# RMS factors of a four-layer transformer: the broadcast copy left out, the squares summed later, and the reciprocal root on GpSimd

## The chip, the core and the metric

The kernel runs on one core of a Trainium2 chip. The core has five engines that work side by side from instruction queues of their own: TensorE (PE) for matmuls, VectorE (DVE), ScalarE (ACT), GpSimd (POOL) and SyncE (SP), which here only starts DMA transfers. The metric is the device time of one execution in microseconds (us); several executions are made, and their median counts.

## What is computed

Four transformer layers run over 512 tokens of width 1024, in float32. Two are hybrid layers, whose mixer joins chunked attention, a convolution module and a retention branch; two are layers with latent attention, whose two low-rank projections (ckv and cq) have RMS norms of their own. Every layer has an FFN of squared ReLU. What matters here is that each layer is framed by norms:

```python
def rms_norm(x, g):
    y = xf * lax.rsqrt(jnp.mean(xf * xf, axis=-1, keepdims=True) + EPS)
    return (y * g.astype(jnp.float32)).astype(x.dtype)

def hybrid_layer(x, ...):
    h = rms_norm(x, g_mix_pre)
    ...
    mix = jnp.concatenate([y_att, y_conv, y_ret], axis=-1) @ w_out
    x = x + rms_norm(mix, g_mix_post)
    h = rms_norm(x, g_mlp_pre)
    f = jnp.square(jax.nn.relu(h @ w_up)) @ w_down
    return x + rms_norm(f, g_mlp_post)
```

The convolution's and the retention's layer norms need a reciprocal root as well.

## The kernel before

**Layout.** The activations stand transposed: x is 8 tiles of 128 features x 512 tokens, so a norm is a sum over partitions and over 8 tiles. The weights come as chunks of 128x1024 by DMA from SP into `raw` (three buffers). ACT rounds each chunk to `wh` (L510) and DVE subtracts to get the rest, `wl` (L512). Every product is three matmuls: wh with the activation's high part hh, wh with its low part hl, wl with hh (L528 to L530 in `dense`, L545 to L547 in `lin_tok`).

**A norm.** ACT squares each tile and DVE adds the squares into one accumulator (`add_sq`, L676, L677). PE multiplies the accumulator by a column of 1/d, one matmul with one output column for 128 tokens, into a bank pc (L662, "the column sums" here). `rstd` (L629 to L643) makes the reciprocal root y of pc + EPS on DVE: v, a seed by an integer shift (L635, L636), and three Newton steps of three instructions each (L638 to L640): twelve instructions on 128 x 2, 4 or 8 elements. `bcast_rows` copies y, each token's value repeated 128 times, into a tile bt (DVE, L647), and PE transposes bt 128 columns at a time (L653): now the value of each token stands on every partition in a bank rb.

There are 32 such norms in the program. Ten are *factors* (`factor_parts`): the norm ahead of a projection is applied behind it, so the projection runs on x times gain meanwhile, and y is also copied to `rt` (L689) and rb to SBUF by ACT (L692). Ten are *halves*: the mixer's and, in the hybrid layers, the FFN's output is normed in two halves of 256 tokens (eight in `post_norm1`, and two for the program's output). Six are of the retention, two of the convolution, four of the latents ckv and cq.

**post_norm1.** Its `sink` takes each output tile into f (L991) and sums squares into acc. Its `done`, a generator, waits for the norm of a half, and then for each of the 8 tiles: f = f * gain * rb (DVE, L1005), x = x + f (DVE, L1007), the parts hh (ACT, L681) and hl (DVE, L682) of the next projection's input, and the squares of the new x into acc2 (ACT L676, DVE L677) for the factor that comes next. The consumer of hh and hl is the next projection's first half, on PE.

**Order.** The program is written as a stream of Python generators; a scheduler then sets the order of each engine's instructions by its own costs and due times. Each engine runs its own row in order and waits at semaphores. So an instruction that waits holds up what stands behind it on its engine.

Of the kernel before, what the change touches and what calls it, by code (L numbers as in the profile page):

```python
# [13 lines left out]
I32 = mybir.dt.int32  # L14
AF = mybir.ActivationFunctionType
ALU = mybir.AluOpType
# [46 lines left out]
CHAIN = 2  # L63
# [285 lines left out]

CONSTS = ("ident", "one1", "m256", "m64", "tri", "neg1", "identr", "smask", "vec", "cmpv")


class Normed:
# [8 lines left out]
class Prog:  # L364
    def __init__(self, nc, tc, es, A, out, plan):
# [18 lines left out]
        else:  # L384
            self.__dict__.update(dict.fromkeys(CONSTS, nc))
            self.ones = dict.fromkeys((1024, 256, 128), nc)
# [54 lines left out]
    def consts(self):  # L441
        nc, A = self.nc, self.A

        def c(nm, shape, dt=F32):
            return self.cst.tile(shape, dt, tag=nm, name=nm)

        self.ident = c("ident", [128, 128])
        make_identity(nc, self.ident)
        self.ones = {}
        for d in (1024, 256, 128):  # L450
            self.ones[d] = c(f"ones{d}", [128, 1])
            nc.vector.memset(self.ones[d], 1.0 / d)
        self.one1 = c("one1", [128, 1])
        nc.vector.memset(self.one1, 1.0)
        self.m256 = c("m256", [128, 128])
        nc.vector.memset(self.m256, 1.0 / 256)
        self.m64 = c("m64", [128, 128])
        nc.vector.memset(self.m64, 0.0)
        nc.vector.memset(self.m64[0:64, 0:64], 1.0 / 64)
        nc.vector.memset(self.m64[64:128, 64:128], 1.0 / 64)  # L460
        self.tri = c("tri", [128, 128], F32R)
        nc.gpsimd.memset(self.tri.bitcast(F32), -1.0)
        nc.gpsimd.affine_select(self.tri, self.tri, pattern=[[-1, 128]], compare_op=ALU.is_ge,
                                fill=0.0, base=0, channel_multiplier=1)
        self.neg1 = c("neg1", [128, 128], F32R)
        nc.gpsimd.memset(self.neg1.bitcast(F32), -1.0)
        self.identr = c("identr", [128, 128], F32R)
        nc.vector.tensor_copy(self.identr, self.ident)
        self.smask = c("smask", [128, 128], F32R)
        nc.gpsimd.memset(self.smask.bitcast(F32), NEG)  # L470
        nc.gpsimd.affine_select(self.smask, self.smask, pattern=[[-1, 128]], compare_op=ALU.is_ge,
                                fill=0.0, base=0, channel_multiplier=1)

        nc.scalar.activation(c("warm", [128, 1]), self.one1, AF.Copy)
        self.vec = c("vec", [128, NVEC])
        nc.sync.dma_start(self.vec, A["vec"])
        self.cmpv = c("cmpv", [128, 4])
# [151 lines left out]
    def rstd(self, pc, n):  # L629

        nc = self.nc
        v, y, a = (self.SM(x)[:, :n] for x in "vya")
        yi = y.bitcast(I32)
        nc.vector.tensor_scalar(v, pc, EPS, None, op0=ALU.add)
        nc.vector.tensor_scalar(yi, v.bitcast(I32), 1, None, op0=ALU.logical_shift_right)  # L635
        nc.vector.tensor_scalar(yi, yi, -1, 0x5F3759DF, op0=ALU.mult, op1=ALU.add)  # L636
        for _ in range(3):
            nc.vector.tensor_tensor(a, y, y, op=ALU.mult)  # L638
            nc.vector.scalar_tensor_tensor(a, a, -0.5, v, op0=ALU.mult, op1=ALU.mult)
            nc.vector.scalar_tensor_tensor(y, a, 1.5, y, op0=ALU.add, op1=ALU.mult)  # L640
        return y

    def bcast_rows(self, y, nt, g, bank=None):  # L643

        nc = self.nc
        bt = self.S(s="bt")
        nc.vector.tensor_copy(  # L647
            bt[:, :nt * 128].rearrange("p (n r) -> p n r", n=nt * g),
            y.rearrange("p (n o) -> p n o", o=1).to_broadcast([128, nt * g, 128 // g]))
        rb = (bank or self.ptr)(nt * 128)  # L650
        for t in range(nt):
            s = slice(128 * t, 128 * t + 128)
            nc.tensor.transpose(rb[:, s], bt[:, s], self.ident)  # L653
        return rb

    def mean_rstd(self, accs, d, t0=0, t1=512, bank=None):
# [327 lines left out]
    def post_norm1(self, xs, f, g_post, g_next):  # L984

        nc = self.nc
        acc, last, acc2, hd = self.S(s="acc"), self.S(s="last"), self.S(s="acc2"), Normed(self)

        def sink(i, o, ps, t0, t1):
            s = slice(t0, t1)  # L990
            nc.vector.tensor_tensor(f[o][:, s], ps, f[o][:, s], op=ALU.add)  # L991
            if i < 7:
                self.add_sq(acc[:, s], f[o][:, s], i == 0)
            else:
                nc.scalar.activation(last[:, s], f[o][:, s], AF.Square)

        def done(t0, t1):
            s = slice(t0, t1)
            y = self.mean_rstd([acc, last], 1024, t0, t1)
            yield  # L1000
            yield
            rb = self.bcast_rows(y, (t1 - t0) // 128, 1)
            yield
            for o in range(8):
                nc.vector.scalar_tensor_tensor(f[o][:, s], f[o][:, s], g_post[:, o:o + 1], rb,  # L1005
                                               op0=ALU.mult, op1=ALU.mult)
                nc.vector.tensor_tensor(xs[o][:, s], xs[o][:, s], f[o][:, s], op=ALU.add)  # L1007
                self.gained(xs[o], g_next, hd, o, t0, t1)
                self.add_sq(acc2[:, s], xs[o][:, s], o == 0)
                if o % CHAIN == CHAIN - 1:  # L1010
                    yield
            if t1 == 512:
                self.after = self.factor_parts(hd, [acc2], FACTOR_LAG)

        return sink, done, hd

    def residual2(self, xs, scale, g_next, final=False):
# [594 lines left out]
```

## Time and profile before

| | |
|---|---|
| median of 3 runs | 3307.41 us (3305.97 to 3307.50) |
| the profiled execution's own time | 3305.43 us |
| its span on the core | 3303.7 us |
| TensorE's granted clock, mean | 0.994 of full speed |
| PE busy | 3251.5 us, 98% of the span |
| DVE busy | 1964.7 us, 59% |
| ACT busy | 1345.8 us, 41% |
| GpSimd busy | 70.0 us, 2% |

The span is the time from the first to the last instruction of the profiled execution; 1.7 us of that execution lie around it. The page lists busy time of each engine, the chain of work that ended last, and groups of instructions. A timeline row gives the start, the length, the engine, the line of the code, the operation with its output and inputs, and in brackets how long the engine stood idle before it and what released it. Matmuls overlap in PE, so their lengths are longer than the distance of their starts, and the distance is the pace.

### The profile page before, as it was taken

How to read it: one execution, taken by the hardware profiler on the slowest of the kernel's cores; microseconds unless marked ns; L12 is line 12 of the kernel's file. 1: busy time of each engine (PE TensorE's matmuls, PEld its weight loads, DVE VectorE, ACT ScalarE, POOL GpSimd, SP SyncE). 2: the span in 40 equal slices, each digit the busy share in tenths (PEclk: the TensorE clock that was granted, in tenths of full speed). 3: DMA queues.
4: the chain of work that ended last, by engine and by line, in shares of the span. 5: the costliest groups of instructions: out<-in, count | busy, mean ns of one | idle time of the engine just before them, and what ended most of it. 6: DMA issues, size and time to landing. Idle time of an engine off the chain costs nothing.

```text
span 3303.7 us, 40955 instructions
## 1 busy us (share of the span) xinstructions
PE 3251.5 (98%) x15956; PEld 2673.1 (81%) x15956; DVE 1964.7 (59%) x3571; ACT 1345.8 (41%) x2254; POOL 70.0 (2%) x151
## 2 busy tenths in 40 slices
PE   8999999999999999999999999999999999999998
PEld 7888888887888888888877688888888877778887
DVE  6977334788734456454678664546445468664454
ACT  4454323546533333232566732323222357742222
POOL 0100000010000000000000000000000000000000
PEclk9999999999999999999999999999999999999999
DMA  5222222342122222222323032222222323222222
GB/s 176 95 71 89 97 101 96 119 137 83 65 102 96 96 96 101 98 96 96 117 85 120 20 106 99 96 96 96 96 96 97 121 79 106 68 77 96 96 96 70
DMA packets 100866, 317.27 MB, mean 96 GB/s; under 512 B 12608, under 2 KB 18112, under 8 KB 100672
## 3 DMA queue, kind: packets, MB, share of 16 engines
q1 hardware_dynamic: 100672, 314.66, 28.3%
q8 instruction: 125, 2.05, 0.2%
q14 instruction: 69, 0.57, 0.1%
HBM read 298.75 MB, written 6.29 MB: 92 GB/s over the span
## 4 chain that ended last, share of the span: by engine, by line
PE 90%; DVE 5%; ACT 2%; DMA 1%; issue 1%; SPq 0%; DVEq 0%; ACTq 0%
PE pd L528 12%; PE pd L529 12%; PE pd L530 12%; PE ps L530 6%; PE ps L528 6%; PE ps L529 6%; PE pt L528 6%; PE pt L529 6%; PE pt L530 6%; PE po L528 3%; PE po L530 3%; PE po L529 3%; PE po L777 3%; PE pt L745 2%; DVE wl L512 1%; PE ps L617 1%
## 5 line engine op out<-in xcount | busy, mean ns | idle before, releaser
L510 ACT ACTIVATE wh<-raw 128x1024 fp32r<-128x1024 f32 (+2 forms) x546 | 567.5, 1041 | 1356.9 <-PE pd L529 561.2
L512 DVE TENSOR_TENSOR wl<-raw,wh 128x1024 fp32r<-128x1024 f32 (+2 forms) x546 | 654.4, 1200 | 420.0 <-ACT wh L510 418.8
L528 PE MATMUL pd<-hh,wh 128*128 128x512 f32 (+1 forms) x1328 | 506.7, 385 | 7.4 <-ACT wh L510 3.7
L530 PE MATMUL pd<-hh,wl 128*128 128x512 f32 (+1 forms) x1328 | 505.3, 381 | 3.1 <-DVE wl L512 3.1
L529 PE MATMUL pd<-hl,wh 128*128 128x512 f32 (+1 forms) x1328 | 506.2, 382 | 0.4 <-DVE hl L682 0.2
L528 PEld LDWEIGHTS pd<-hh,wh 128*128 128x128 f32 x1328 | 249.0, 189 | 58.9 <-ACT hh L681 5.9
L530 PEld LDWEIGHTS pd<-hh,wl 128*128 128x128 f32 x1328 | 250.8, 189 | 49.1 <-DVE wl L512 3.3
L529 PEld LDWEIGHTS pd<-hl,wh 128*128 128x128 f32 x1328 | 250.9, 189 | 46.7 <-DVE hl L682 2.0
L530 PE MATMUL ps<-hh,wl 128*128 128x512 f32 (+1 forms) x528 | 196.7, 374 | 0.0
L529 PE MATMUL ps<-hl,wh 128*128 128x512 f32 (+1 forms) x528 | 196.3, 372 | 0.0
L528 PE MATMUL ps<-hh,wh 128*128 128x512 f32 (+1 forms) x528 | 196.1, 373 | 0.2 <-ACT wh L510 0.2
L528 PE MATMUL pt<-hh,wh 128*128 128x512 f32 x480 | 187.1, 391 | 0.6 <-ACT wh L510 0.6
L529 PE MATMUL pt<-hl,wh 128*128 128x512 f32 x480 | 187.3, 390 | 0.0
L530 PE MATMUL pt<-hh,wl 128*128 128x512 f32 x480 | 186.3, 389 | 0.0
L528 PE MATMUL pd<-ah,wh 128*128 128x512 f32 (+1 forms) x498 | 185.0, 372 | 0.0
L529 PE MATMUL pd<-al,wh 128*128 128x512 f32 (+1 forms) x498 | 184.8, 371 | 0.0
L530 PE MATMUL pd<-ah,wl 128*128 128x512 f32 (+1 forms) x498 | 184.8, 371 | 0.0
L586 ACT ACTIVATE ah<-sc 128x512 fp32r<-128x512 f32 x88 | 55.6, 632 | 180.9 <-DVE sc L1130 180.9
L529 PE MATMUL ps<-al,wh 128*128 128x512 f32 (+1 forms) x332 | 123.4, 372 | 0.0
L528 PE MATMUL pt<-ah,wh 128*128 128x512 f32 (+1 forms) x332 | 123.3, 371 | 0.0
L530 PE MATMUL ps<-ah,wl 128*128 128x512 f32 (+1 forms) x332 | 123.3, 371 | 0.0
L530 PE MATMUL pt<-ah,wl 128*128 128x512 f32 (+1 forms) x332 | 123.2, 371 | 0.0
(475 smaller groups left out, 6354.5 us busy)
## 6 DMA issues: line engine op xcount, KB each, us to landing
raw<-in_w SPq DMA_DIRECT2D x514, 512.0 KB
raw<-in_w SPq DMA_DIRECT2D x20, 384.0 KB
xd<-x SPq DMA_DIRECT2D x16, 256.0 KB
x<-xd SPq DMA_DIRECT2D x16, 256.0 KB
sw<-sc SPq DMA_DIRECT2D x48, 64.0 KB
ct<-in_ret SPq DMA_DIRECT2D x12, 256.0 KB
sn<-in_ret SPq DMA_DIRECT2D x12, 256.0 KB
mst<-in_bias SPq DMA_DIRECT2D x12, 256.0 KB
```

The lines of the kernel that those rows point to most:

```text
L510: nc.scalar.activation(h[:, :n], raw[:, :n], AF.Copy)
L512: eng.tensor_tensor(lo[:, :n], raw[:, :n], h[:, :n].bitcast(F32), op=ALU.subtract)
L528: mm(ps, h, rh[j][:, t0:t1], start=first and j == 0, stop=False)
L529: mm(ps, h, rl[j][:, t0:t1], start=False, stop=False)
L530: mm(ps, lo, rh[j][:, t0:t1], start=False, stop=last and j == n - 1)
L586: self.nc.scalar.activation(dst, src, AF.Copy, scale=scale)
L617: self.nc.tensor.matmul(ps, st, m[:, c], start=True, stop=False)
L745: nc.tensor.transpose(pt[:, o:o + 128], P[qt][:, 128 * kt:128 * kt + 128], self.ident)
L777: self.nc.tensor.matmul(po[a:a + 64, 128 * kt:512], v[kt][:, o + a:o + a + 64], pt[kt], start=start and kt == 0, stop=stop and kt == 3, sk ...
```

## The change

The functions `rstd`, `bcast_rows` and `post_norm1.done` change, and a constant tile of -0.5 (128x8) is added.

- `rstd`: v = pc + EPS stays on DVE. The root is then one GpSimd instruction, v to the power -0.5, and one Newton step follows on GpSimd in four instructions. Eleven DVE instructions go, five GpSimd instructions come, in all 32 norms.
- `bcast_rows`: for a norm with one group per token (26 of 32; the six retention norms have two groups) the copy bt goes. PE's transpose reads y itself, one column repeated 128 times.
- `post_norm1.done`: the squares of the new x are summed in a loop of their own behind the eight tiles, not tile by tile.

```diff
-CONSTS = ("ident", ...
+CONSTS = ("mhalf", "ident", ...
...
+        self.mhalf = c("mhalf", [128, 8])
+        nc.vector.memset(self.mhalf, -0.5)
...
         v, y, a = (self.SM(x)[:, :n] for x in "vya")
-        yi = y.bitcast(I32)
         nc.vector.tensor_scalar(v, pc, EPS, None, op0=ALU.add)
-        nc.vector.tensor_scalar(yi, v.bitcast(I32), 1, None, op0=ALU.logical_shift_right)
-        nc.vector.tensor_scalar(yi, yi, -1, 0x5F3759DF, op0=ALU.mult, op1=ALU.add)
-        for _ in range(3):
-            nc.vector.tensor_tensor(a, y, y, op=ALU.mult)
-            nc.vector.scalar_tensor_tensor(a, a, -0.5, v, op0=ALU.mult, op1=ALU.mult)
-            nc.vector.scalar_tensor_tensor(y, a, 1.5, y, op0=ALU.add, op1=ALU.mult)
+        nc.gpsimd.tensor_tensor(y, v, self.mhalf[:, :n], op=ALU.pow)
+        nc.gpsimd.tensor_tensor(a, y, y, op=ALU.mult)
+        nc.gpsimd.tensor_tensor(a, a, v, op=ALU.mult)
+        nc.gpsimd.tensor_scalar(a, a, -0.5, 1.5, op0=ALU.mult, op1=ALU.add)
+        nc.gpsimd.tensor_tensor(y, y, a, op=ALU.mult)
         return y
...
-        bt = self.S(s="bt")
-        nc.vector.tensor_copy(
-            ...
         rb = (bank or self.ptr)(nt * 128)
+        if g > 1:
+            bt = self.S(s="bt")
+            nc.vector.tensor_copy(
+                ...
         for t in range(nt):
             s = slice(128 * t, 128 * t + 128)
-            nc.tensor.transpose(rb[:, s], bt[:, s], self.ident)
+            nc.tensor.transpose(rb[:, s], bt[:, s] if g > 1 else y[:, t:t + 1].to_broadcast([128, 128]), self.ident)
...
                 self.gained(xs[o], g_next, hd, o, t0, t1)
+                if o % CHAIN == CHAIN - 1:
+                    yield
+            for o in range(8):
                 self.add_sq(acc2[:, s], xs[o][:, s], o == 0)
-                if o % CHAIN == CHAIN - 1:
+                if o % 4 == 3:
                     yield
```

The scheduler gives the new code a new order. The FFN bodies keep theirs; around the norms it changes. DVE's row goes from 3555 to 3178 instructions, GpSimd's from 123 to 287. This table, counted from the two orders, says how many matmuls stand on PE between a norm's last column sum and its first transpose (norms numbered in the order of the program):

| norms | before | after |
|---|---|---|
| factors 1; 8, 18, 21; 11 | 27; 30; 39 | 5; 8; 12 |
| factors 22, 27; 25, 30; 26 | 23; 25; 17 | 8; 8; 4 |
| first halves of a mixer 6, 16; of an FFN 9, 19 | 47; 43 | 24; 30 |
| second halves 7, 17; 10; 20 | 33; 49; 38 | 9; 6; 14 |
| halves of the output 31; 32 | 26; 0 | 11; 0 |
| ckv 23, 28; cq 24, 29 | 10; 20 | 4; 7 |
| conv 5; 15 | 19; 16 | 8; 8 |
| retention 2, 12; 3, 13; 4; 14 | 47; 47; 58; 48 | 26; 8; 31; 23 |

On PE at the ckv norm of the first latent layer (norm 23), before. `pd` is the bank of the norm, L617 and L618 transpose a state, L1249 applies attention weights:

```order
L662 MATMUL pd_13902<-ones_91,acc_13820 128x1 x4
L617 MATMUL ps_13943<-mh_13481,st_13730 128x128
L618 MATMUL ps_13943<-ml_13482,st_13730 128x128
L617 MATMUL pt_13954<-mh_13487,st_13733 128x128
L618 MATMUL pt_13954<-ml_13488,st_13733 128x128
L1249 MATMUL po_13641<-a_13889,v_13440 64x512
L1249 MATMUL po_13641<-a_13900,v_13440 64x512
L617 MATMUL ps_13971<-mh_13481,st_13730 128x256
L618 MATMUL ps_13971<-ml_13482,st_13730 128x256
L617 MATMUL pt_13982<-mh_13487,st_13733 128x256
L618 MATMUL pt_13982<-ml_13488,st_13733 128x256
L653 MATMUL pd_13924<-ident,bt_13922 128x128 x4
```

and after (lines of the changed kernel, one to four lines higher):

```order
L663 MATMUL pd_13740<-ones_91,acc_13658 128x1 x4
L619 MATMUL ps_13773<-mh_13319,st_13568 128x128
L620 MATMUL ps_13773<-ml_13320,st_13568 128x128
L619 MATMUL pt_13784<-mh_13325,st_13571 128x128
L620 MATMUL pt_13784<-ml_13326,st_13571 128x128
L654 MATMUL pd_13754<-ident,y_13746 128x128 x4
L1253 MATMUL po_13479<-a_13727,v_13278 64x512
L1253 MATMUL po_13479<-a_13738,v_13278 64x512
```

The transposes, which read y in place of bt, stand behind 4 matmuls in place of 10.

On DVE at the factor behind the mixer of layer 0 (norm 8), before. v to y are `rstd`, wl the rests of weight chunks:

```order
L634 TENSOR_SCALAR v_2850<-po_2845 128x4
L635 TENSOR_SCALAR y_2851<-v_2850 128x4
L636 TENSOR_SCALAR y_2851<-y_2851 128x4
L638 TENSOR_TENSOR a_2852<-y_2851 128x4
L639 SCALAR_TENSOR_TENSOR a_2852<-a_2852,v_2850 128x4
L640 SCALAR_TENSOR_TENSOR y_2851<-a_2852,y_2851 128x4
L638 TENSOR_TENSOR a_2852<-y_2851 128x4
L639 SCALAR_TENSOR_TENSOR a_2852<-a_2852,v_2850 128x4
L512 TENSOR_TENSOR wl_2686<-raw_2683,wh_2685 128x1024
L512 TENSOR_TENSOR wl_2744<-raw_2741,wh_2743 128x1024
L640 SCALAR_TENSOR_TENSOR y_2851<-a_2852,y_2851 128x4
L512 TENSOR_TENSOR wl_2942<-raw_2939,wh_2941 128x1024
```

(the last Newton step, rt and bt follow) and after:

```order
L635 TENSOR_SCALAR v_2802<-po_2797 128x4
L690 COPY rt_2176<-y_2803 128x4
L514 TENSOR_TENSOR wl_2634<-raw_2631,wh_2633 128x1024
L514 TENSOR_TENSOR wl_2680<-raw_2677,wh_2679 128x1024
L1106 SCALAR_TENSOR_TENSOR relu_2854<-pd_2542,rb_2175 128x512
L1106 SCALAR_TENSOR_TENSOR relu_2861<-pd_2543,rb_2175 128x512
L1106 SCALAR_TENSOR_TENSOR relu_2868<-ps_2544,rb_2175 128x512
```

Behind v stands at once `rt`, which reads the y of GpSimd; two wl that stood inside the norm's instructions stand behind it, and then the FFN's squared ReLU (L1106), which reads rb.

On DVE behind the mixer's first half in layer 0, before. acc_421 is acc2, the squares of the new x; acc_2188 is acc, those of f in the second half:

```order
L682 SCALAR_TENSOR_TENSOR hl_2201<-x_120,vec,hh_2193 128x256
L1005 SCALAR_TENSOR_TENSOR f_2100<-f_2100,vec,pt_2436 128x256
L677 TENSOR_TENSOR acc_421_2190<-acc_421_2190,sq_2489 128x256
L682 SCALAR_TENSOR_TENSOR hl_2202<-x_121,vec,hh_2194 128x256
L1007 TENSOR_TENSOR x_122<-x_122,f_2100 128x256
L677 TENSOR_TENSOR acc_421_2190<-acc_421_2190,sq_2496 128x256
L677 TENSOR_TENSOR acc_2188<-acc_2188,sq_2513 128x256
L682 SCALAR_TENSOR_TENSOR hl_2203<-x_122,vec,hh_2195 128x256
L1005 SCALAR_TENSOR_TENSOR f_2137<-f_2137,vec,pt_2436 128x256
L677 TENSOR_TENSOR acc_421_2190<-acc_421_2190,sq_2520 128x256
L1007 TENSOR_TENSOR x_123<-x_123,f_2137 128x256
L991 TENSOR_TENSOR f_1846<-po_2530,f_1846 128x256
```

and after:

```order
L1006 SCALAR_TENSOR_TENSOR f_2068<-f_2068,vec,pt_2396 128x256
L678 TENSOR_TENSOR acc_2156<-acc_2156,sq_2438 128x256
L683 SCALAR_TENSOR_TENSOR hl_2169<-x_122,vec,hh_2161 128x256
L1008 TENSOR_TENSOR x_124<-x_124,f_2068 128x256
L683 SCALAR_TENSOR_TENSOR hl_2170<-x_123,vec,hh_2162 128x256
L1006 SCALAR_TENSOR_TENSOR f_2105<-f_2105,vec,pt_2396 128x256
L678 TENSOR_TENSOR acc_2156<-acc_2156,sq_2463 128x256
L683 SCALAR_TENSOR_TENSOR hl_2171<-x_124,vec,hh_2163 128x256
L1008 TENSOR_TENSOR x_125<-x_125,f_2105 128x256
L992 TENSOR_TENSOR f_1822<-po_2474,f_1822 128x256
L1006 SCALAR_TENSOR_TENSOR f_2126<-f_2126,vec,pt_2396 128x256
L683 SCALAR_TENSOR_TENSOR hl_2172<-x_125,vec,hh_2164 128x256
```

The sums into acc2 have gone from between f, x and hl; in the changed program they stand behind the last hl of the half.

## Rows read from the trace of the kernel before

**Rows 1.** The page, section 1 (busy us, share of the span, instructions) and 4 (chain).
```profile
PE 3251.5 (98%) x15956; PEld 2673.1 (81%) x15956; DVE 1964.7 (59%) x3571; ACT 1345.8 (41%) x2254; POOL 70.0 (2%) x151
...
PE 90%; DVE 5%; ACT 2%; DMA 1%; issue 1%; SPq 0%; DVEq 0%; ACTq 0%
```

**Rows 2.** Timeline of PE; start us, us, engine line op out<-in [idle before <-releaser].
```profile
611.77 0.28 PE L530 MATMUL pd<-ah,wl 128*128 128x256 f32 x1
611.89 0.28 PE L528 MATMUL pd<-ah,wh 128*128 128x256 f32 x1
...
3292.83 0.61 PE L662 MATMUL pt<-ones,acc 128*128 128x1 f32 x4 [1.88 <-DVE acc L677]
3296.27 0.66 PE L653 MATMUL pt<-ident,bt 128*128 128x128 f32 x2 [2.84 <-DVE bt L647]
```

**Rows 3.** Windows: length, busy us (count) of PE PEld DVE ACT POOL, PEclk, DMA share, GB/s.
```profile
246.00:262.40 16.40, 13.98 (x93) 11.95 (x91) 16.00 (x41) 9.44 (x22) 0.00 (x0) 0.92 0.11 40
262.40:270.40 8.00, 8.00 (x52) 8.00 (x53) 5.08 (x20) 0.32 (x1) 0.00 (x0) 0.74 0.39 133
858.00:875.00 17.00, 15.40 (x97) 13.27 (x95) 16.38 (x41) 9.77 (x24) 0.00 (x0) 0.88 0.13 46
875.00:883.00 8.00, 8.00 (x46) 8.00 (x47) 4.43 (x18) 0.00 (x0) 0.00 (x0) 0.62 0.40 131
617.00:621.00 4.00, 3.98 (x15) 3.98 (x16) 4.00 (x10) 1.24 (x3) 0.00 (x0) 0.65 0.63 197
```

**Rows 4.** View of line L653, idle of its engine before it (us, times).
```profile
  DVE bt L647: 9.8, 14
```

**Rows 5.** Timeline of DVE at the program's last norm.
```profile
3293.47 0.16 DVE L634 TENSOR_SCALAR v<-pt 128x2 f32<-128x2 f32 x1 [0.31 <-PE pt L662]
...
3295.83 0.29 DVE L647 COPY bt<-y 128x256 f32<-128x256 f32 x1
```

**Rows 6.** Timeline where GpSimd follows DVE.
```profile
1636.80 0.29 DVE L1222 SCALAR_TENSOR_TENSOR e<-ps,e 128x128 f32<-128x128 f32 x1 [2.15 <-ACT e L1221]
...
1637.22 0.29 POOL L1223 TENSOR_SCALAR_AFFINE_SELECT e<-e 128x128 f32<-128x128 f32 x1 [52.28 <-DVE e L1222]
```

**Rows 7.** Timeline of GpSimd (POOL) at the start of the program.
```profile
0.40 0.10 POOL L1603 MEMSET const-uint8-127<- 128x1 uint8 x1
...
2.07 0.29 POOL L471 TENSOR_SCALAR_AFFINE_SELECT smask<-smask 128x128 fp32r<-128x128 f32 x1
2.42 1.09 POOL L606 MEMSET ml<- 64x512 f32 x2
```

**Rows 8.** Groups of GpSimd by line and shape: xcount, busy us, mean ns, idle before.
```profile
L825 POOL TENSOR_SCALAR_AFFINE_SELECT st<-st 128x128 f32<-128x128 f32 x48 | 27.8, 602 | 210.7 <-ACT st L578 206.2 <-DVE st L580 3.2 <-DVE a L639 1.1
```

**Rows 9.** Timeline of GpSimd and DVE together in a mixer.
```profile
84.26 2.38 POOL L825 TENSOR_SCALAR_AFFINE_SELECT st<-st 128x128 f32<-128x128 f32 x4 [0.86 <-ACT st L578]
84.34 2.15 DVE L882 SCALAR_TENSOR_TENSOR cv<-cy,vec,cv 128x512 f32<-128x512 f32 x3
```

**Rows 10.** Timeline of PE at three waits behind halves.
```profile
257.35 0.50 PE L528 MATMUL pd<-hh,wh 128*128 128x256 f32 x2 [0.93 <-ACT hh L681]
...
617.02 0.44 PE L547 MATMUL ps<-wl,hh 128*128 128x384 f32 x1 [2.83 <-DVE wl L512]
...
1230.53 0.39 PE L530 MATMUL pd<-hh,wl 128*128 128x256 f32 x1 [3.08 <-DVE wl L512]
```

**Rows 11.** Timeline of DVE behind the mixer's first half, layer 0.
```profile
256.94 0.47 DVE L1005 SCALAR_TENSOR_TENSOR f<-f,vec,pt 128x256 f32<-128x256 f32 x1
257.33 0.48 DVE L682 SCALAR_TENSOR_TENSOR hl<-x,vec,hh 128x256 fp32r<-128x256 f32 x1
257.73 0.42 DVE L1007 TENSOR_TENSOR x<-x,f 128x256 f32<-128x256 f32 x1
258.07 0.42 DVE L677 TENSOR_TENSOR acc<-acc,sq 128x256 f32<-128x256 f32 x1
```

**Rows 12.** The page, section 5: a group's busy us, mean ns, idle time before it, releaser.
```profile
L512 DVE TENSOR_TENSOR wl<-raw,wh 128x1024 fp32r<-128x1024 f32 (+2 forms) x546 | 654.4, 1200 | 420.0 <-ACT wh L510 418.8
```

More of the change, by code (lines that the diff above doesn't have):

```diff
@@ L348, in _tables @@
     return {k: np.ascontiguousarray(v, dtype=f) for k, v in tabs.items()}
-CONSTS = ("ident", "one1", "m256", "m64", "tri", "neg1", "identr", "smask", "vec", "cmpv")
+CONSTS = ("mhalf", "ident", "one1", "m256", "m64", "tri", "neg1", "identr", "smask", "vec", "cmpv")
 class Normed:
@@ L645, in bcast_rows @@
         nc = self.nc
-        bt = self.S(s="bt")
-        nc.vector.tensor_copy(
-            bt[:, :nt * 128].rearrange("p (n r) -> p n r", n=nt * g),
-            y.rearrange("p (n o) -> p n o", o=1).to_broadcast([128, nt * g, 128 // g]))
         rb = (bank or self.ptr)(nt * 128)
+        if g > 1:
+            bt = self.S(s="bt")
+            nc.vector.tensor_copy(
+                bt[:, :nt * 128].rearrange("p (n r) -> p n r", n=nt * g),
+                y.rearrange("p (n o) -> p n o", o=1).to_broadcast([128, nt * g, 128 // g]))
         for t in range(nt):
             s = slice(128 * t, 128 * t + 128)
-            nc.tensor.transpose(rb[:, s], bt[:, s], self.ident)
+            nc.tensor.transpose(rb[:, s], bt[:, s] if g > 1 else y[:, t:t + 1].to_broadcast([128, 128]), self.ident)
         return rb
```

## The prediction

> **What bounds the kernel now.** I read the page's busy line and its chain of waits first. PE is busy for 3251.5 of 3303.7 us, the chain is 90% PE and 5% DVE, and GpSimd (POOL) has 70 us of work [rows 1]. So a microsecond counts only if PE stands still in it, and DVE's lighter load (the change takes some 380 small instructions from it) counts only where PE waits for DVE. Next I took PE's pace from its timeline: a 256-column matmul starts every 0.12 us (611.77, 611.89) [rows 2], and one of 512 takes at most two of these. With that pace, a window shows what PE lost in it: count times pace, against its length. Four windows follow the norms of the mixer's output and of the FFN's output [rows 3]: 93 matmuls at 0.12 are 11.2 us in a window of 16.4 us, so 5.2 are lost, and 97 in 17.0 us lose 5.4; in both, DVE is busy nearly throughout. The granted clock is 0.74 and 0.62 in the 8 us behind them, where 52 and 46 matmuls (6.2 and 5.5 us) lose 1.8 and 2.5 us. Last, I asked who waits for the step that the change touches. The view of the transposes' own line has 9.8 us of idle time before them until the copy bt (L647) was there [rows 4]; PE's matmuls and weight loads are counted apart there, so that one wait can stand in it twice, and I take 7.5 us as what the norms cost PE today. It is so little because the order puts 10 to 58 matmuls between a norm's column sums and its transposes; the one bare place is the end of the program (2.84 us at 3296.27 [rows 2]).
>
> **The new chain's length.** From the last column sum to the transposes, on a quiet DVE. Of four column sums that start 0.11 apart from 3292.83 on, the last starts at 3293.16, and v at 3293.47: 0.3 us [rows 2, 5]. v itself lasts 0.16. DVE to GpSimd: an instruction ending at 1637.09 frees one that starts at 1637.22, 0.1 [rows 6]. Then five dependent GpSimd instructions on 128x4. No row shows one of these, a power least of all. The nearest rows: a memset of 128x1 takes 0.10, an affine_select of 128x128 0.29, and there are 0.06 us between the end of one (2.07 + 0.29) and the start of the next (2.42) [rows 7]. An instruction on 4 columns must pay at least the first of these; I take 0.2 for four of them, and 0.4 for the power, which has more to compute per element: 1.2, with four gaps 1.44 us. Last, 0.15 from the end of the operand (bt, 3295.83 + 0.29) to the transpose (3296.27) [rows 2, 5]. Sum S = 2.15 us. Bounds: all five at the memset's 0.10 give 1.45; four at 0.29 with the power 1 us longer than 0.4 give 3.5. Before, twelve DVE instructions 0.197 apart (3293.47 to 3295.83) and bt took 2.65 us [rows 5] against 1.7 now from v to the end of the fifth, so the chain in itself gets shorter.
>
> **What it costs: the order moves, too.** The program's order now places the transposes only 0 to 14 matmuls behind the sums in 24 of 32 norms (the table of the change). There PE stalls for S, less the cover that these matmuls give at PE's pace, less 0.11 for the last sum itself. On a quiet DVE: seven factors with 8 matmuls of 256 columns, 4 of 512 or 5 mixed (0.91 to 0.96 of cover) lose 1.1 each, 7.6; two ckv norms with 4 matmuls of 128 columns (0.44) lose 1.6 each, 3.2; the last two halves (11 matmuls of 256 and none) lose 0.7 and 2.0. Sum 13.5. At the busy places GpSimd waits for DVE as well: the same affine_select takes 0.602 on average beside DVE's traffic against 0.29 alone [rows 7, 8], and at 84.3 four of them took 2.38 us while three DVE instructions ran 2.15 us [rows 9], so about one GpSimd instruction passes per DVE instruction, and the chain becomes five DVE instructions of 0.33 to 1.2 us long. With covers of 0.9 to 2.9 us I count: two retention norms 1.1 each, two convs 0.6, second halves 1.8 twice (9 matmuls), 1.65 and 1.35, first halves 0.2 twice, cq 1.15 twice, the two factors with wl ahead of v 1.0 each. Sum 14.7. Together 28.2, less the 7.5 that the norms cost today: **+20.7 us**. Each 0.1 us of S is worth 2.5 us.
>
> VectorE is the engine for elementwise work and GpSimd takes about twice its time, says the Trainium skill ("GPSIMD Engine Reference", sections 3.1, elementwise, and 4.1, engine selection); the rows above, on small tiles, show 0.1 to 0.29 against DVE's 0.16 to 0.29 [rows 5, 7], so not a factor of two throughout. By that rule the sum would come out as in the third rival below.
>
> **What it gives.** First, the stretch after the mixer's first half. PE waits there for hh, 0.93 us at 257.35 [rows 10], because hh needs x and x stands in DVE's row among f (0.39), x (0.33), hl (0.40) and the square sums (0.33, like x) [rows 11]. The late squares take 7 sums out (2.3 us) and the transposes stand 23 matmuls (2.8 us) earlier against PE's work. End to end DVE then has 8 x (0.39 + 0.33 + 0.40) + 10 x 0.335 + 2 wl of 1.2 [rows 12], 14.7 us, beside 13.9 us of matmuls. I leave 1.5 lost in each of the two layers: 5.2 + 5.4 - 3.0 = 7.6 gained. The half clock behind them (1.8 + 2.5) goes with the idle stretch; I take 4.0 of 4.3. Second, after an FFN's first half PE waits 2.83 and 3.08 us for a wl (L512) that stands on DVE behind the same row of f, x, hl and sums [rows 10]. Now DVE has 6 f, 6 x, 5 hl and 7 additions ahead of that wl (three quarters of a chunk, 0.9), 9.6 us, and with 13 more matmuls behind the transposes PE has 83 x 0.12, 10.0 us; with the way there and back I leave 0.25 each, so 5.4, and with the window behind the first (15 matmuls of 384 columns, at one and a half times 0.12, are 2.7 in 4.0 us at clock 0.65 [rows 3]; 1.3), 6.7. Sum 7.6 + 4.0 + 6.7: **-18.3 us**. The late sums cost nothing: in the second half DVE has 8 f, x and hl (9.0 us), 8 sums (2.7) and 2 wl (2.4), 14.1 us behind the transposes, and PE comes to the column sums after 125 matmuls of 0.12, 15.0 us. The copy's removal on DVE is worth nothing elsewhere, since PE had cover there.
>
> **Sum.** 20.7 - 18.3 = +2.4 on the profiled execution's 3305.4: 3307.8. The median of the runs shown is 2 us above it, so the forecast is **3309 us**, within 0.2% (6.6 us, about what a measurement of this kernel can tell from no change).
>
> **Rivals.**
> - GpSimd's small instructions cost what its smallest row costs (0.10, power included): S = 1.45, 0.7 less than taken; at 2.5 us per 0.1 that would be 17 us, and I take 13, since at the busy places DVE sets the pace. That gives 2.4 - 13 = -10.6, with the median 3297. For it: four memsets on one column in the rows; against it: they read nothing, and a power reads two operands.
> - Slower: the power is 1 us longer than taken. S = 3.1, +25 over the forecast, 3334. It decides by 0.2% from a chain 0.2 us longer than taken. The place to see it is ckv, where 4 short matmuls cover nothing. No row speaks against it, since none shows a power.
> - Each GpSimd step costs twice DVE's spacing, 0.39: S = 2.65, 0.5 more than taken, +12, 3321. The 0.10 and 0.29 [rows 7] speak against it, the 0.602 [rows 8] for it. It is what the page of the Trainium skill named above would make of this chain.
> - The late squares and the earlier transposes give only half, since hh and x stay bound by DVE's f and hl: -9 instead of -18.3, 3318. For it: DVE keeps 14.7 us of work in a stretch of 13.9.
>
> **How the numbers follow.** Forecast (within 0.2%) 0.37; cheap chain 0.22; long power 0.14; twice DVE 0.10; half the gain 0.12; cheap chain and all of the gain with the quiet places covered (below 3296) 0.05. Faster by over 0.2%: 0.27, slower: 0.36, within: 0.37. The range takes the cheap chain and the long power in, 3296 to 3335; outside it stay a power of 2 us and the last case.
>
> **What would show it.** In the new trace: the row of the power and of the four steps behind it (0.4 and 0.2); PE's waits for GpSimd at the transposes, about 1.1 us at a factor and 1.6 at ckv, 24 of them; the windows of [rows 3] shorter by 3 to 4 us each, at clock 1.0; the waits for wl of 2.83 and 3.08 gone. I am wrong if the power is below 0.15 or above 0.8 us, if the same affine_select on a busy DVE is no guide to tensor_tensor, or if PE still waits for hh in the first halves.

## The result and the profile after

The changed kernel takes 3331.93 us (median of 4 runs, 3330.92 to 3334.51) against 3307.45 for the kernel before: the ratio is 1.0077, with a 95% interval of 1.0066 to 1.0089. It is slower by 24.5 us. The forecast was no change, 3309. The range, 3296 to 3335, holds the time, near its upper end; the nearest of the cases is the rival of the long power, 3334, which had a chance of 0.14.

The page of the changed kernel, sections 1 and 4, beside [rows 1]:

```profile
PE 3251.3 (98%) x15956; PEld 2674.8 (80%) x15956; DVE 1912.6 (57%) x3194; ACT 1345.9 (40%) x2254; POOL 138.9 (4%) x311
...
PE 46%; issue 44%; DVE 5%; POOL 2%; ACT 2%; DMA 1%; SPq 0%; DVEq 0%; POOLq 0%; ACTq 0%
```

PE does the same work in the same busy time and the span is 26.8 us longer (3330.5), so by the page PE stands still that much more. DVE has 52 us less to do, and the span doesn't show it. GpSimd's busy time has doubled and 2% of the chain is on it. The chain's "issue" share says little: it is time for which the profile shows no wait.

PE's list of waits (us in total, times, longest us), its first five lines:

```profile
PE po L654 <- POOL y L640: 13.2, 10, 1.5
PE pt L654 <- POOL y L640: 10.4, 8, 2.1
PE pt L654 <- DVE bt L649: 8.9, 4, 2.5
PE ps L547 <- ACT wh L512: 7.8, 1, 7.8
PE pd L654 <- POOL y L640: 6.1, 4, 2.0
```

All but the fourth (the first weight chunk, there before as well) are the transposes, 38.6 us. The same list of the kernel before has 5.6 for them ([rows 4] has 9.8 because weight loads are counted in):

```profile
PE pt L653 <- DVE bt L647: 3.7, 3, 2.8
...
PE pd L653 <- DVE bt L647: 1.4, 2, 0.7
...
PE po L653 <- DVE bt L647: 0.5, 3, 0.2
```

The group view of GpSimd (xcount, busy us, mean ns, idle before) points at the cause:

```profile
L636 POOL TENSOR_TENSOR y<-v,mhalf 128x4 f32<-128x4 f32 x16 | 19.1, 1195 | 1480.5 <-DVE v L635 1424.3 <-DVE st L726 56.2
L636 POOL TENSOR_TENSOR y<-v,mhalf 128x8 f32<-128x8 f32 x6 | 15.3, 2544 | 86.2 <-DVE v L635 79.0 <-DVE st L721 7.1
L636 POOL TENSOR_TENSOR y<-v,mhalf 128x2 f32<-128x2 f32 x10 | 9.6, 963 | 850.0 <-DVE v L635 850.0
L638 POOL TENSOR_TENSOR a<-a,v 128x4 f32<-128x4 f32 x16 | 3.2, 201 | 1.3
```

L636 is the power. It takes 1.2 us on average on 4 columns and 2.5 on 8, where a multiplication on the same tile takes 0.20. The timeline of one factor (norm 22) on a quiet DVE shows the whole chain, to be held against [rows 5]:

```profile
1615.22 0.58 PE L663 MATMUL po<-ones,acc 128*128 128x1 f32 x4
...
1615.85 0.16 DVE L635 TENSOR_SCALAR v<-po 128x4 f32<-128x4 f32 x1 [1.15 <-PE po L663]
1616.09 1.01 POOL L636 TENSOR_TENSOR y<-v,mhalf 128x4 f32<-128x4 f32 x1 [344.45 <-DVE v L635]
1617.17 0.20 POOL L637 TENSOR_TENSOR a<-y 128x4 f32<-128x4 f32 x1
1617.45 0.20 POOL L638 TENSOR_TENSOR a<-a,v 128x4 f32<-128x4 f32 x1
1617.74 0.19 POOL L639 TENSOR_SCALAR a<-a 128x4 f32<-128x4 f32 x1
1618.02 0.20 POOL L640 TENSOR_TENSOR y<-y,a 128x4 f32<-128x4 f32 x1
...
1618.27 0.54 PE L654 MATMUL po<-ident,y 128*128 128x128 f32 x3 [1.40 <-POOL y L640]
```

From the last column sum's start (1615.56) to the transposes 2.71 us pass; 8 matmuls of 256 columns cover 0.96 of it and PE waits for the rest. The matmuls that the order leaves between a norm's column sums and its transposes are called its cover below, and what PE still waits its stall.

**Where the time went.** To split the loss, I took for each matmul the distance to the next one's start, less the pace of its shape (0.227, 0.174, 0.120, 0.109 us for 512, 384, 256, 128 columns), and put the excess in three boxes: ahead of a norm's first transpose; in stretches of half granted clock, up to one pace per matmul; all the rest. The kernels of the experiments stand in the same table. The boxes and the half-clock time (some 2 us of it behind the last instruction) are those of the one profiled execution of each kernel, whose time lies up to 3.7 us from the median (e10, 3293.02).

| kernel | ahead of transposes | half clock | rest | half-clock time | median us |
|---|---|---|---|---|---|
| before | 8.3 | 11.1 | 121.3 | 38.8 | 3307.45 |
| changed | 43.1 | 16.0 | 107.5 | 52.7 | 3331.93 |
| e1 GpSimd alone | 40.8 | 18.6 | 117.3 | 59.3 | 3338.94 |
| e2 without GpSimd | 10.7 | 9.1 | 120.7 | 29.8 | 3304.34 |
| e3 late squares alone | 12.3 | 10.4 | 121.0 | 33.8 | 3308.28 |
| e4 no copy alone | 8.3 | 8.9 | 120.9 | 30.9 | 3304.58 |
| e5 no power | 22.6 | 8.2 | 106.2 | 28.8 | 3302.56 |
| e6 no Newton step | 21.5 | 6.0 | 106.9 | 21.4 | 3299.36 |
| e7 later transposes | 42.3 | 12.8 | 100.7 | 39.5 | 3321.46 |
| e8 squares early again | 40.0 | 16.7 | 116.6 | 53.4 | 3336.76 |
| e9 copy back | 39.5 | 13.8 | 110.5 | 46.0 | 3328.18 |
| e10 e6 and e7 | 18.7 | 4.2 | 105.7 | 19.3 | 3296.73 |

For the change: +34.8, +4.9 and -13.9, together +25.8; the first matmul also starts 0.9 us later, which gives the 26.7 between the two last matmuls.

### The profile page after: what moved, and what is told of

It reads as the page before. It is cut to its first block, busy times and chain, and to the rows that moved or that the text cites. A ratio compares the mean times of both kernels' runs of the same rounds, so it can differ in the third digit from the quotient of the medians.

```text
span 3330.5 us, 40741 instructions
## 1 busy us (share of the span) xinstructions
PE 3251.3 (98%) x15956; PEld 2674.8 (80%) x15956; DVE 1912.6 (57%) x3194; ACT 1345.9 (40%) x2254; POOL 138.9 (4%) x311
## 4 chain that ended last, share of the span: by engine, by line
PE 46%; issue 44%; DVE 5%; POOL 2%; ACT 2%; DMA 1%; SPq 0%; DVEq 0%; POOLq 0%; ACTq 0%
PE pd L530 7%; PE pd L531 6%; PE pd L532 6%; PE po L778 2%; PE pt L530 2%; PE pt L531 2%; PE pt L532 2%; PE ps L532 2%; PE ps L531 2%; PE ps L530 2%; PE pt L746 2%; POOL y L636 1%; DVE cv L883 1%; PE ps L619 1%; PE po L531 1%
## 5 line engine op out<-in xcount | busy, mean ns | idle before, releaser
L636 POOL TENSOR_TENSOR y<-v,mhalf 128x4 f32<-128x4 f32 (+2 forms) x32 | 44.0, 1376 | 2416.7 <-DVE v L635 2353.4
L530 PE MATMUL ps<-ah,wh 128*128 128x512 f32 (+1 forms) x332 | 123.4, 372 | 0.0
L531 PE MATMUL pt<-al,wh 128*128 128x512 f32 (+1 forms) x332 | 123.2, 371 | 0.0
```

The costliest lines, as they stand in the source:

```text
L530: mm(ps, h, rh[j][:, t0:t1], start=first and j == 0, stop=False)
L531: mm(ps, h, rl[j][:, t0:t1], start=False, stop=False)
L636: nc.gpsimd.tensor_tensor(y, v, self.mhalf[:, :n], op=ALU.pow)
```

## The experiments

Each experiment ran with the kernel before beside it, whose median was 3306.38 for e1 to e4, 3306.00 for e5 to e7 and 3305.45 for e8 to e10. Ratios are to that; a difference of a few us between medians of different groups is firm only if it holds there as well.

**e1: the root on GpSimd alone.** The kernel before with the new `rstd` and the constant tile; the copy and the early squares stay.

```diff
-        nc.vector.tensor_scalar(yi, v.bitcast(I32), 1, None, op0=ALU.logical_shift_right)
...
+        nc.gpsimd.tensor_tensor(y, v, self.mhalf[:, :n], op=ALU.pow)
+        nc.gpsimd.tensor_tensor(a, y, y, op=ALU.mult)
...
```

> The root on GpSimd alone: power and Newton step as in the changed kernel, but the copy bt is kept and the squares stay in the tile loop. Theory (the loss is the GpSimd chain, 2.7 us from sums to transposes with the power at 1.0 us, behind covers of 5 to 13 matmuls): bt adds 0.4 us to the chain and the covers are only 1 to 4 matmuls longer, so about +30 us on the kernel before, 3337 us. Rival (the loss comes from the late squares or the missing copy, GpSimd costs about nothing): within 5 us of 3307.

Measured: 3338.94, ratio 1.0096 (1.0081 to 1.0111), 33 us over the kernel before beside it. GpSimd's part alone carries the loss and more than it.

**e2: everything but GpSimd.** The changed kernel with the twelve DVE instructions back in `rstd`.

> The changed kernel with the root on DVE again (twelve instructions); the copy stays out and the squares stay late. Theory (GpSimd chain is the loss, the other two parts bring what the trace of the changed kernel shows, about 10 us): 3297 us, 35 us under the changed kernel. Rival (the other two parts carry the loss): 3315 or more. My prediction's gain of 18 us in full would give 3289.

Measured: 3304.34, ratio 0.9994 (0.9985 to 1.0003), so no difference that can be told. The loss is gone, as the theory had it, but the 10 us of gain that it expected didn't come: the rest box is 120.7, as before. So what the changed kernel gains in the rest box (13.9 us) doesn't belong to late squares and missing copy by themselves.

**e3 and e4: late squares alone, copy left out alone.** Each on the kernel before.

```diff
             for o in range(8):
...
+                if o % CHAIN == CHAIN - 1:
+                    yield
+            for o in range(8):
                 self.add_sq(acc2[:, s], xs[o][:, s], o == 0)
-                if o % CHAIN == CHAIN - 1:
+                if o % 4 == 3:
                     yield
```

```diff
+        if g > 1:
...
-            nc.tensor.transpose(rb[:, s], bt[:, s], self.ident)
+            nc.tensor.transpose(rb[:, s], bt[:, s] if g > 1 else y[:, t:t + 1].to_broadcast([128, 128]), self.ident)
```

> Late squares alone, copy and DVE chain as before. If the gain in the stretches behind the first halves is that of the 7 sums that leave them (2.3 us each, four of them, less half), 3302 us; second half 10 has no matmul between sums and transposes, which costs up to 3 us of it. If the gain comes only from the transposes' earlier place, no change: 3307.

> The copy left out alone, squares early, DVE chain. The first halves' transposes stand 13 to 15 matmuls earlier. If the earlier place is what gains in those stretches, 3300 us; if it is the squares' leaving, 3306 (bt's 0.3 us at the last norm and some tenths at ckv).

Measured: 3308.28, ratio 1.0000 (0.9990 to 1.0009), and 3304.58, ratio 0.9992 (0.9983 to 1.0001). Neither can be told from no change; the expected gains of 5 and 7 us are not there.

**e5: the power out, the order kept.** The power becomes a multiplication of the same shape, so the root itself is left out; PE's, DVE's and ACT's rows are word for word those of the changed kernel.

```diff
-        nc.gpsimd.tensor_tensor(y, v, self.mhalf[:, :n], op=ALU.pow)
+        nc.gpsimd.tensor_tensor(y, v, self.mhalf[:, :n], op=ALU.mult)
...
-        nc.gpsimd.tensor_scalar(a, a, -0.5, 1.5, op0=ALU.mult, op1=ALU.add)
-        nc.gpsimd.tensor_tensor(y, y, a, op=ALU.mult)
+        nc.gpsimd.tensor_scalar(a, a, 0.0, 0.2, op0=ALU.mult, op1=ALU.add)
+        nc.gpsimd.tensor_tensor(y, a, a, op=ALU.mult)
```

> The changed kernel in its own order, with the power replaced by a multiplication of v by the constant (and the last two GpSimd steps made to give a constant, so every norm factor is a constant: the norms are left out in value, not in work). Theory (the power's time is the price): each power shrinks from 1.01 (4 columns), 0.70 (2) and 2.0 (8) to 0.2 to 0.33; taken off each place's stall down to zero that is 25 of the 43 us at the transposes: 3306 us. Rival (the price is the way to GpSimd and back, and the order): no more than half of that, 3319 or more.

Measured: 3302.56, ratio to the kernel before 0.9992 (0.9982 to 1.0001), 29 us under the changed kernel. Its group rows of L636:

```profile
L636 POOL TENSOR_TENSOR y<-v,mhalf 128x8 f32<-128x8 f32 x6 | 6.6, 1103 | 87.4 <-DVE v L635 80.3 <-DVE st L721 7.2
L636 POOL TENSOR_TENSOR y<-v,mhalf 128x4 f32<-128x4 f32 x16 | 6.1, 382 | 1472.9 <-DVE v L635 1417.8 <-DVE st L726 55.1
L636 POOL TENSOR_TENSOR y<-v,mhalf 128x2 f32<-128x2 f32 x10 | 4.6, 460 | 850.6 <-DVE v L635 850.6
```

0.8 us shorter on 4 columns and 1.4 on 8, on average. At the transposes 20.5 us are won of the 25 expected; half clock gives 7.9 more, which the expectation didn't count. With the rest of the kernel unmoved, the power's time is shown to be the price. What stays without it, 14.3 us more at the transposes than in the kernel before, is about what the rest box gives back (15.1).

**e6: no Newton step.** The power alone makes the root.

```diff
         nc.gpsimd.tensor_tensor(y, v, self.mhalf[:, :n], op=ALU.pow)
-        nc.gpsimd.tensor_tensor(a, y, y, op=ALU.mult)
-        nc.gpsimd.tensor_tensor(a, a, v, op=ALU.mult)
-        nc.gpsimd.tensor_scalar(a, a, -0.5, 1.5, op0=ALU.mult, op1=ALU.add)
-        nc.gpsimd.tensor_tensor(y, y, a, op=ALU.mult)
```

> The changed kernel without the Newton step: the power alone on GpSimd (the root is as exact as the power). The chain is 1.04 us shorter (2.72 to 1.68 us on a quiet DVE). The order draws the transposes nearer by about the same work, from 8 matmuls of cover to 4 at factors, from 4 to 2 at ckv. Theory (the order takes back what the chain gives, stall is chain less cover): about 0.6 us per place is won, 13 us in all, 3319. Rival (only the chain's length counts): 25 us, 3307.

Measured: 3299.36, ratio to the kernel before 0.9981 (0.9971 to 0.9990): faster than both kernels. The theory's 3319 was wrong. Its formula holds at the factors. Here is norm 22 again:

```profile
1592.38 0.16 DVE L635 TENSOR_SCALAR v<-po 128x4 f32<-128x4 f32 x1 [1.15 <-PE po L659]
1592.69 1.01 POOL L636 TENSOR_TENSOR y<-v,mhalf 128x4 f32<-128x4 f32 x1 [345.15 <-DVE v L635]
...
1593.75 0.65 PE L650 MATMUL po<-ident,y 128*128 128x128 f32 x4 [0.82 <-POOL y L636]
```

The wait has gone from 1.40 to 0.82, 0.6 as expected, since the order took four of the eight matmuls away. But most second halves and the retention norms kept nearly all their cover and won 0.9 to 1.1 us each, so the transposes' box falls by 21.6 and not by 13; and the half clock's box by 10.

**e7: the transposes later in the second halves.** The order on GpSimd is the changed kernel's.

```diff
             y = self.mean_rstd([acc, last], 1024, t0, t1)
-            yield
-            yield
+            for _ in range(4 if t0 else 2):
+                yield
```

> The changed kernel with two more yields between sums and transposes in the second halves: at norms 7 and 17 there are 26 matmuls in place of 9, at 20 it is 32 in place of 14, at 10 still 6; all else alike. Theory (stall is chain less cover, and each such stall is followed by half clock): 2.0, 2.0 and 1.1 us go at the transposes, and the half clock behind 269 us goes too, 3 us: 3324. Rival (the later start of the second half is paid at the factors 8, 18, 21, which need its squares): 3332.

Measured: 3321.46, ratio to the kernel before 1.0048 (1.0033 to 1.0063), 10.5 us under the changed kernel (9 when each is held against the kernel before beside it), better than expected, but not as expected. The stalls at norms 7, 17 and 20 fall from 2.0, 2.0 and 1.1 us to 0.8, 0.8 and 0; factors 8, 18 and 11 take that back (1.6 to 2.5, 1.6 to 2.5, 0.4 to 1.8), since more of DVE's work now lies in their chain. Here is factor 8:

```profile
284.06 1.01 POOL L636 TENSOR_TENSOR y<-v,mhalf 128x4 f32<-128x4 f32 x1 [14.85 <-DVE v L635]
...
284.21 2.36 DVE L514 TENSOR_TENSOR wl<-raw,wh 128x1024 fp32r<-128x1024 f32 x2 [0.23 <-ACT wh L512]
...
285.14 0.34 POOL L637 TENSOR_TENSOR a<-y 128x4 f32<-128x4 f32 x1
...
285.57 1.06 POOL L638 TENSOR_TENSOR a<-a,v 128x4 f32<-128x4 f32 x1
```

The transposes' box ends at 42.3. The gain is in the rest box (-6.8) and the half clock (-3.2). So the rival's cost was real, and the theory had the wrong place for the gain; why the rest box falls stays open.

**e8 and e9: one part of the change undone.** The squares back in the tile loop, and the copy back in; GpSimd's chain stays in both.

> The changed kernel with the squares back in the tile loop; GpSimd's chain stays and the copy stays out. PE's time lost elsewhere than at the transposes is 13.9 us less in the changed kernel than before, but only 0.6 less with the root on DVE (e2). Theory (the late squares bring it, once the short chain has drawn the transposes forward): most of the 13.9 comes back, 3340. Rival (the transposes' place brings it alone): 3333, as changed.

> The changed kernel with the copy bt back; GpSimd's chain and late squares stay. The first halves' transposes then stand 47 and 43 matmuls behind the sums, as before the change, in place of 24 and 30. Theory (the transposes' earlier place brings the 13.9 us): most of it comes back, 3340 or more. Rival (the late squares bring it): 3334.

Measured: 3336.76, ratio to the kernel before 1.0091 (1.0077 to 1.0105), and 3328.18, ratio 1.0067 (1.0054 to 1.0081). Without the late squares 9.1 of the 13.9 us in the rest box come back. With the copy, whose first halves have 47 and 43 matmuls of cover again, the rest box keeps 10.8 of its gain. So late squares bring the rest box's gain, but only with the root on GpSimd (e3 and e2 show nothing), and the early place of the transposes, on which my prediction built, isn't needed for it. Why they need the root on GpSimd stays open: that DVE's row is shorter by eleven instructions per norm is a candidate, and no run tells it apart. Whether leaving the copy out costs this kernel anything can't be told: e9 lies 3.8 us under the changed kernel, but 1.8 when each is held against the kernel before beside it, and the two intervals overlap. In the boxes the transposes fall by 3.6 with the copy (the second halves 7 and 17 have 22 matmuls of cover in place of 9), the half clock by 2.2, and the rest rises by 3.0.

**e10: e6 and e7 together.**

> The changed kernel without the Newton step (e6) and with the later transposes in the second halves (e7). If the two gains add (32.6 and 10.5 us on the changed kernel's 3332), 3289. If the later place was worth its gain only to a long chain, about 3298, as e6 alone: e6 has only 1.0 us of stall left at norms 7 and 17 and none at 20.

Measured: 3296.73, ratio to the kernel before 0.9971 (0.9960 to 0.9982), the fastest here, 0.3% under the kernel before and 1% under the changed one. The gains don't add: it lies 2.6 us under e6, or 2.1 when each is held against the kernel before beside it, and the two intervals overlap, so that e7's change adds anything to e6 is not shown. That is close to the second expectation; 3289 lies outside the interval. PE's waits for the power in it:

```profile
PE po L650 <- POOL y L636: 7.0, 9, 0.8
...
PE pd L650 <- POOL y L636: 2.6, 4, 1.1
PE pt L650 <- POOL y L636: 2.0, 2, 1.1
```

11.6 us stay at 15 places, most of them with 2 to 7 matmuls of cover.

## Where the prediction failed and where it was right, step by step

**The chain's length: the failing term is one number.** "0.4 for the power" measured 1.01 on 4 columns with a quiet DVE and 0.70 on 2. The other terms held within 0.1: 0.29 to v, 0.16 for v, 0.08 to GpSimd, four steps of 0.20, gaps of 0.08, 0.05 to the transposes. S is 2.71 to 2.73 at the quiet 4-column places in place of 2.15, and 0.6 of it is the power. The bound, 1.4, held it, and the prediction's own sign of being wrong, a power above 0.8 us, came. e5, which takes the power out and leaves the rest, shows that this term makes the loss. I had no row of a power, and took a value near the cheap end because the nearest rows were cheap; a value in the middle of the bounds, 0.75, would have given 3318, slower.

**Chain less cover is what PE waits.** That step was right. With 0.57 more chain the factors stall 1.6 us (forecast 1.1), ckv 2.1 (1.6), the last halves 0.9 and 2.3 (0.7 and 2.0), the convs 0.7 (0.6), the first halves nothing (0.2). Factor 11, which the sum left out, stalls 0.4. No run keeps the covers of before (23 to 30 matmuls at most factors) with the power in, so whether the change would have been free with them is not shown; the first halves, with 24 and 30, lost nothing.

**The busy places were taken too cheap where the power meets DVE.** The same 128x4 power beside a wl:

```profile
1928.78 0.16 DVE L635 TENSOR_SCALAR v<-po 128x4 f32<-128x4 f32 x1
1928.91 1.23 DVE L514 TENSOR_TENSOR wl<-raw,wh 128x1024 fp32r<-128x1024 f32 x1
1929.03 1.98 POOL L636 TENSOR_TENSOR y<-v,mhalf 128x4 f32<-128x4 f32 x1 [109.31 <-DVE v L635]
1931.08 0.20 POOL L637 TENSOR_TENSOR a<-y 128x4 f32<-128x4 f32 x1
```

The power is lengthened by about the wl's time, 1.98 for 1.01, and the steps behind it run freely. "One GpSimd instruction per DVE instruction", read from [rows 9], was right for a GpSimd instruction that starts while such a DVE instruction runs, and the factors 25 and 30 stall 1.6 us for 1.0. A wl that starts later didn't lengthen the power (1.01 in e7's rows). The retention norms show the largest miss. Their power has 8 columns and takes 2.0 to 3.25 us, and behind it stands bt: two with 8 matmuls of cover stall 2.6 us each (forecast 1.1), and two with 31 and 23, which I had down as covered, 1.8 and 2.5. Here are one of the first pair and the last of them:

```profile
756.28 0.63 PE L654 MATMUL pt<-ident,bt 128*128 128x128 f32 x4 [2.45 <-DVE bt L649]
...
795.11 1.11 PE L654 MATMUL pt<-ident,bt 128*128 128x128 f32 x4 [2.35 <-DVE bt L649]
```

In sum the transposes cost +34.8 us where the forecast said +20.7.

**The rule of the Trainium skill** ("GPSIMD Engine Reference", sections 3.1 and 4.1), GpSimd at half of DVE's speed, would have given each step 0.39. The Trainium skill gives that factor there for operations with two inputs and has it from tiles of N = 2048. Here the plain steps took 0.20 and started 0.28 apart, where DVE's started 0.197 apart [rows 5], a factor of 1.4, so it doesn't hold on tiles of 2 and 4 columns. The 3321 that it gives is nearer to the result than my forecast only because four steps too dear and one power too cheap nearly cancel.

**The gains without the clock: right in sum, half wrong in place.** Of 18.3 us, 5.3 were clock and 13.0 waits; the rest box shows 13.9. Counted from the transposes of one norm to those of the next, the mixers' first halves give 4.6 of the 7.6, and the FFN halves with what follows them 3.2 of the 5.4: in layer 1 they win 2.5, in layer 0 0.7, since PE still waits 1.22 us for a wl at 623.42 (2.83 before) and loses 0.9 more behind the second half. Windows of the changed kernel that answer to [rows 3], the first half in layer 0 and what follows, then layer 1 (length, busy us (count) of PE, PEld, DVE, ACT, POOL, PEclk, DMA share, GB/s):

```profile
250.20:264.30 14.10, 13.74 (x107) 12.92 (x106) 13.81 (x34) 7.92 (x17) 0.00 (x0) 1.00 0.22 76
264.30:269.30 5.00, 3.90 (x27) 3.21 (x25) 4.60 (x10) 3.56 (x11) 1.71 (x2) 1.00 0.26 93
269.30:276.10 6.80, 5.82 (x27) 5.82 (x28) 5.09 (x15) 1.63 (x4) 0.68 (x4) 0.50 0.27 89
...
875.00:890.00 15.00, 14.42 (x107) 13.10 (x106) 14.87 (x36) 9.53 (x23) 0.60 (x1) 1.00 0.19 69
890.00:898.00 8.00, 6.13 (x52) 5.93 (x51) 6.15 (x17) 2.59 (x8) 1.78 (x5) 1.00 0.35 125
```

The first row is the gain as forecast: 107 matmuls are 12.8 us at 0.12, and 1.3 are lost in place of 5.2. Rows two and three give part of it back: the second half's power waits beside a wl, PE stands for 1.86 us at 270.28, and the clock is at half. The other 6 us of the rest box came at places that the forecast didn't name: 2.9 in the latent layers' mixers, 2.7 in the attention, convolution and retention of the two hybrid layers, 1.3 in the second halves of the mixers; the start of the program loses 0.8.

**The clock went the other way.** I let the half-clock stretches go with the stalls that precede them in [rows 3]: -5.3. They went up, +4.9, most likely because the change makes new stalls. Before the tail there are five such stretches in the kernel before and ten in the changed one, and seven of these ten lie within or right behind a stall of 1.6 to 2.6 us at the transposes (at 269.3, 631.1, 757.4, 794.9, 911.0, 1685.8 and 2290.0). Many such stalls have none behind them, so a stall alone doesn't decide it. But where the runs took much of the stalls away (e5, e6, e10) the half-clock time fell to 28.8, 21.4 and 19.3 us. The direction holds over executions, the size is that of one: the mean granted clock was 0.992 to 0.993 in all four of the changed kernel, and from 0.991 to 0.997, mostly 0.994 to 0.996, in those of the kernel before.

**The sum, and the rivals.** With the transposes at +34.8 in place of +20.7 (14.1) and the clock at +4.9 in place of -5.3 (10.2), the two steps make up the miss of some 23 us. The rival "the power is 1 us longer" had S = 3.1 and 3334; the power was 0.6 longer, and clock and busy places did the rest, so that 3334 comes so near is in part luck. Its point of decision, a chain 0.2 us longer than taken, was passed by far. The range held the time, 3296 to 3335, and its upper end was that rival. "The copy's removal is worth nothing" held as far as can be told: neither e4 nor e9 shows a difference that is clear of the noise, though the order draws the transposes nearer when the copy isn't there.

## What to carry to other kernels

Before moving a short dependent chain to another engine, count the work that the order leaves between its first and last link, because the order may close the gap as the chain is reckoned shorter; what PE waits is chain less cover. An instruction of a kind that no row shows is safer taken near the middle of its bounds than near the cheap rows around it; here that would have turned the forecast the right way. And a part that is worth nothing alone (late squares, e3) can save 9 us of PE's waits beside another (e8), so undo parts one at a time from the changed kernel as well as adding them to the kernel before.

## What the runs showed of the hardware

- GpSimd's float32 power on 128 partitions took 0.70 us on 2 columns and 1.01 on 4, so about 0.4 and 0.155 per column by these two sizes; on 8 columns, always beside DVE's work here, 2.0 to 3.25. Multiplications, and multiply-add by constants, on tiles of 2 and 4 columns took 0.19 to 0.20 where DVE left them alone, with 0.08 between dependent ones.
- A GpSimd instruction that started while a DVE subtraction of 1.2 us ran grew by about what was left of it: the power from 1.01 to 1.98, and e5's multiplication at the same place from 0.20 to 1.16, with 1.1 left. A subtraction that started 0.15 us behind the power left it at 1.01 (e7, 284.06).
- PE's transposes read one column, repeated 128 times, as their stationary operand at no extra cost: a row of three took 0.54 us at 1618.27, and the line's median is 0.273 with y as with bt in the changed kernel.
- In the changed kernel's half-clock stretch at 757.4 (granted clock 0.50, 1.2 GHz) matmuls of 512 columns started 0.43 us apart (758.76, 759.19, 759.61), against 0.23 at full clock.
